# A decoder trunk on one core: dense matmuls in closed runs of twelve

## The chip, the cores and the metric

The kernel runs on one core of a Trainium2 chip. The metric is the device time of one execution in microseconds, the median of several runs. TensorE multiplies matrices into PSUM banks; VectorE, ScalarE and GpSimd compute elementwise; SyncE issues the DMAs that bring the weights.

## What is computed

The reference is a trunk of two residual layers, each followed by a dense FFN, over 512 tokens of width 1024 in float32. Cut to its frame:

```python
for i in range(DEPTH):                      # DEPTH = 2
    if i % 2 == 0:                          # SSD heads and GLA heads from one input projection
        h = rms_norm(x, mix_norm_even[j])
        proj = h @ w_in                     # z, xbc, dt, q, k, v, g, gk_low
        x = x + concat(ssd_mixer(...), gla_mixer(...)) @ w_out
    else:                                   # multi-head latent attention, 16 heads, causal
        h = rms_norm(x, mix_norm_odd[j])
        x = x + mla_layer(h, w_dqkv, ..., w_o)
    x = x + (silu(h2 @ w_gate) * (h2 @ w_up)) @ w_down     # h2 = rms_norm(x, ffn_norm[i])
```

The SSD part has 16 heads of 64 with chunks of 128 tokens, the GLA part 4 heads with chunks of 64, the hidden width of the FFN is 2816.

## The kernel before

The activations lie transposed, width on the 128 partitions and the 512 tokens along the free axis, so x is eight tiles X[0..7]. A float32 product is made of three matmuls in a reduced type (`mm3`, L149 to L152): operand and weight are each split into a high and a low part, and high x high (L150), low operand x high weight (L151) and high operand x low weight (L152) are summed in one PSUM bank. `dense` (L154) does this for the eight k tiles of a product, which makes 24 matmuls 128x512 into one bank `acc`. Of these banks there are NACC = 3, taken in turn, so the fourth product after a given one has to wait until that one's bank was read out.

Weights come one block of 512 KB at a time: a DMA into `wraw` (2 buffers), a cast on ScalarE into the high part `whi` (L144), a subtraction on VectorE into the low part `wlo` (L145); whi and wlo have 3 buffers each. `weight` (L130) asks for them under a raised priority of AHEAD = 90.

The order of every engine's instructions is set by the Tile scheduler: it goes by priority, which falls in the order of the program and is raised inside `tc.high_priority(offset=...)`, and by its own estimate of when inputs are there. Products therefore interleave: while a dense product runs, small matmuls of other parts (transposes, scores of a chunk, sums over partitions) can stand between any two of its 24.

The places that the prediction goes through:

- `rstd` (L173 to L197) makes the factor R of a norm. The squares are split (L178, L179), two matmuls with a matrix of ones sum them over the partitions (L181 and L182), and then VectorE works through L186 to L196. All evacuations of the FFN's gate and up products need R (L680, L683).
- `out_round(r)` (L267) adds one quarter of the output product of the first layer, with four parts mxh/mxl as operands. The second quarter takes the SSD's second group, normalized by `group_norm` (L460): y = y x gain x Rg (L464), then a cast mxh (L126) and a subtraction mxl (L127). It is called inside the first GLA head, ahead of that head's scores (L594).
- `conv` (L351) of the SSD part evacuates its product at L358; the recursion dp (L322) shares VectorE with it.
- `attend` (L898) does two heads: scores (L911), mask and maximum (L914), exp (L916), reciprocal (L919), scaling (L922), transposes (L925), copies (L929), and the product with the values (L934) after the last copy. `o_round` (L944) is the output product that runs beside the later heads.
- `ffn` (L666): 22 pairs of a gate and an up product, then the down products.

Of the kernel before, what the change touches and what calls it, by code (L numbers as in the profile page):

```python
# [21 lines left out]
KD = 8  # L22
HID = 2816
KH = HID // P
EPS = 1e-6
AHEAD = 90
VALUES = (2, 3, 7)
SC = 4
NACC = 3
# [17 lines left out]
def kernel(ctx: ExitStack, tc: tile.TileContext, A, yT, stop=99):  # L47
    nc = tc.nc
    V, S, G, E = nc.vector, nc.scalar, nc.gpsimd, nc.tensor
# [47 lines left out]
    ps = acc()  # L97
# [48 lines left out]
        return (hi[:, :kc * m].rearrange("p (k m) -> p k m", k=kc),  # L146
                lo[:, :kc * m].rearrange("p (k m) -> p k m", k=kc))

    def mm3(out, ah, al, bh, bl, first, last):  # L149
        E.matmul(out, ah, bh, start=first, stop=False)  # L150
        E.matmul(out, ah, bl, start=False, stop=False)  # L151
        E.matmul(out, al, bh, start=False, stop=last)  # L152

    def dense(ps, w, xs):  # L154

        n = len(xs)
        for k, (xh, xl) in enumerate(xs):
            mm3(ps, w[0][:, k, :], w[1][:, k, :], xh, xl, k == 0, k == n - 1)

    def rsqrt(pool, m, shape, tag, ytag=""):  # L160

# [124 lines left out]
    with tc.tile_pool(name="gkp", bufs=1) as gkp:  # L286
        rtok = tok_scalar(R)

        ps = aux("a1")
# [15 lines left out]
        ps = aux()  # L305
# [40 lines left out]
        with tc.tile_pool(name="ssd", bufs=2) as sp:  # L346
# [123 lines left out]
            def values(h):  # L470

                wv = [weight(A["w_v"][h, j], 4, 256) for j in range(2)]
                v = gkp.tile([P, 4, 256], F32, name=f"v{h}")
                for i in range(4):
                    ps = acc()
                    for k in range(KD):
                        wh, wl = wv[k // 4]
                        xh, xl = xp[k]
                        mm3(ps[:, :256], xh[:, i * P:(i + 1) * P], xl[:, i * P:(i + 1) * P],
                            wh[:, k % 4, :], wl[:, k % 4, :], k == 0, k == KD - 1)  # L480
                    S.activation(v[:, i, :], ps[:, :256], AF.Copy, scale=rtok[:, i:i + 1])
                vt[h] = v

# [229 lines left out]
    with tc.tile_pool(name="mla", bufs=2) as mp, tc.tile_pool(name="mla1", bufs=1) as m1:  # L713
# [112 lines left out]
        def project(g):  # L826


            qs = mp.tile([P, 4, 4, 96], F32, tag="qs", name=nm("qs"))
            wqs = [weight(A["w_uq"][g, :, k0:k0 + n], n, 384) for k0, n in ((0, 2), (2, 1))]  # L830
            for i in range(4):
                ps = acc()
                for k in range(3):
                    lh, ll = lora["q"][k]
                    wh, wl = wqs[k // 2]
                    mm3(ps[:, :384], lh[:, i * P:(i + 1) * P], ll[:, i * P:(i + 1) * P],
                        wh[:, k % 2, :], wl[:, k % 2, :], k == 0, k == 2)
                S.activation(qs[:, i].rearrange("p h d -> p (h d)"), ps[:, :384], AF.Copy,
                             scale=cf["q"][:, i:i + 1])

            wkv = weight(A["w_ukv"][g], 2, 512)
            ks = mp.tile([P, 4, 4, 64], F32, tag="ks", name=nm("ks"))
            v = mp.tile([P, 4, 4, 64], F32, tag="v", name=nm("v"), bufs=3)
            for i in range(4):
                ps = acc()
                for k in range(2):
                    lh, ll = lora["kv"][k]
                    mm3(ps, lh[:, i * P:(i + 1) * P], ll[:, i * P:(i + 1) * P],
                        wkv[0][:, k, :], wkv[1][:, k, :], k == 0, k == 1)
                p3 = ps.rearrange("p (w h d) -> p w h d", w=2, h=4)  # L850
                S.activation(ks[:, i], p3[:, 0], AF.Copy, scale=cf["kv"][:, i:i + 1])
                S.activation(v[:, i], p3[:, 1], AF.Copy, scale=cf["kv"][:, i:i + 1])

            sq = mp.tile([P, 16, 96], F32, tag="sq", name=nm("sq"), bufs=1)
            st = mp.tile([P, 3, 16], F32, tag="st", name=nm("st"))
            S.activation(sq, qs.rearrange("p i h d -> p (i h) d"), AF.Square)
            V.tensor_reduce(st[:, 0], sq[:, :, 0:64], AX.X, ALU.add)
            V.tensor_reduce(st[:, 1], sq[:, :, 64:96], AX.X, ALU.add)
            S.activation(sq[:, :, 0:64], ks.rearrange("p i h d -> p (i h) d"), AF.Square)
            V.tensor_reduce(st[:, 2], sq[:, :, 0:64], AX.X, ALU.add)  # L860
            for j, n in enumerate((64, 32, 64)):
                V.tensor_scalar(st[:, j], st[:, j], 1.0 / n, EPS, ALU.mult, ALU.add)
            rf = rsqrt(mp, st, [P, 3, 16], "hr")
            q2 = qs.rearrange("p i h d -> p (i h) d")
            V.tensor_tensor(q2[:, :, 0:64], q2[:, :, 0:64],
                            rf[:, 0].unsqueeze(2).to_broadcast([P, 16, 64]), ALU.mult)
            rr = mp.tile([P, 16, 32], F32, tag="rr", name=nm("rr"), bufs=1)
            V.tensor_tensor(rr, q2[:, :, 64:96],
                            rf[:, 1].unsqueeze(2).to_broadcast([P, 16, 32]), ALU.mult)
            rope(qs[:, :, :, 64:96], rr.rearrange("p (i h) d -> p i h d", i=4), tabs[0], [P, 4, 4, 32])  # L870
            k2 = ks.rearrange("p i h d -> p (i h) d")
            V.tensor_tensor(k2, k2, rf[:, 2].unsqueeze(2).to_broadcast([P, 16, 64]), ALU.mult)
            return qs, ks, v
# [184 lines left out]
```

## Time and profile before

| | |
|---|---|
| median of 3 runs | 1372.63 us (1371.01 to 1373.25) |
| the profiled execution's own time | 1371.09 us |
| its span | 1368.9 us |
| TensorE busy | 1344.9 us, 98% |
| VectorE busy | 815.5 us, 60% |
| ScalarE busy | 562.8 us, 41% |

The span is what the trace covers; the time of the execution has some two microseconds around it. Matmuls overlap in the records, so that TensorE's time is read from the distance of one start to the next and not from a record's length. The program in stages, by the trace: the SSD part until about 240 us, GLA heads and output product until 410, the first FFN until 775, the attention layer's projections until 835, its heads until 992, the output product until about 1005, then the second FFN.

### The profile page before, as it was taken

How to read it: one execution, taken by the hardware profiler on the slowest of the kernel's cores; microseconds unless marked ns; L12 is line 12 of the kernel's file. 1: busy time of each engine (PE TensorE's matmuls, PEld its weight loads, DVE VectorE, ACT ScalarE, POOL GpSimd, SP SyncE). 2: the span in 40 equal slices, each digit the busy share in tenths (PEclk: the TensorE clock that was granted, in tenths of full speed). 3: DMA queues.
4: the chain of work that ended last, by engine and by line, in shares of the span. 5: the costliest groups of instructions: out<-in, count | busy, mean ns of one | idle time of the engine just before them, and what ended most of it. 6: DMA issues, size and time to landing. Idle time of an engine off the chain costs nothing.

```text
span 1368.9 us, 16667 instructions
## 1 busy us (share of the span) xinstructions
PE 1344.9 (98%) x6506; PEld 1088.7 (80%) x6506; DVE 815.5 (60%) x1369; ACT 562.8 (41%) x941; POOL 7.8 (1%) x35
## 2 busy tenths in 40 slices
PE   8999999999999999999999999999999999999998
PEld 5788889788888888888888887666588888888887
DVE  7987976788867444444333469776594444443221
ACT  5584633544344322332232348775653322322121
POOL 0000000000000000000000000000000000000000
PEclk9999999999999999999999999999999999999999
DMA  5342232222233333223333321111033223323331
GB/s 177 109 141 91 77 95 78 78 77 62 79 93 105 93 94 106 92 92 99 90 100 100 101 68 56 39 47 62 1 98 103 93 93 102 98 93 108 111 103 63
DMA packets 36781, 122.22 MB, mean 89 GB/s; under 512 B 4768, under 2 KB 5792, under 8 KB 36704
## 3 DMA queue, kind: packets, MB, share of 16 engines
q1 hardware_dynamic: 35888, 120.72, 28.1%
q8 instruction: 51, 0.84, 0.2%
q10 hardware_dynamic: 816, 0.46, 0.1%
q14 instruction: 26, 0.21, 0.0%
HBM read 119.03 MB, written 2.13 MB: 89 GB/s over the span
## 4 chain that ended last, share of the span: by engine, by line
PE 90%; DVE 5%; ACT 3%; issue 1%; DMA 1%; SPq 0%; ACTq 0%
PE acc L150 27%; PE acc L151 27%; PE acc L152 27%; PE sco L911 2%; PE ptr L925 1%; PE po L934 1%; DVE wlo L145 1%; PE a L447 1%; PE a L625 0%; PE a L433 0%; PE a L614 0%; PE a L451 0%; ACT whi L144 0%; PE a L627 0%; DVE gm L534 0%
## 5 line engine op out<-in xcount | busy, mean ns | idle before, releaser
L150 PE MATMUL acc<-xh,whi 128*128 128x512 f32 x1144 | 449.1, 393 | 5.2 <-DVE dp L322 2.5
L144 ACT CAST whi<-wraw 128x1024 fp32r<-128x1024 f32 (+2 forms) x221 | 225.8, 1022 | 554.0 <-PE acc L151 436.9
L151 PE MATMUL acc<-xl,whi 128*128 128x512 f32 x1144 | 448.7, 392 | 0.0
L152 PE MATMUL acc<-xh,wlo 128*128 128x512 f32 x1144 | 448.7, 392 | 0.0
L145 DVE TENSOR_TENSOR wlo<-wraw,whi 128x1024 fp32r<-128x1024 f32 (+2 forms) x221 | 261.9, 1185 | 163.2 <-ACT whi L144 163.1
L150 PEld LDWEIGHTS acc<-xh,whi 128*128 128x128 f32 x1144 | 214.9, 188 | 51.2 <-ACT cvt L366 2.8
L152 PEld LDWEIGHTS acc<-xh,wlo 128*128 128x128 f32 x1144 | 215.1, 188 | 44.8 <-DVE wlo L145 0.6
L151 PEld LDWEIGHTS acc<-xl,whi 128*128 128x128 f32 x1144 | 215.1, 188 | 44.5 <-issue 1.4
L152 PE MATMUL acc<-fhh,wlo 128*128 128x512 f32 x288 | 112.0, 389 | 0.0
L150 PE MATMUL acc<-fhh,whi 128*128 128x512 f32 x288 | 112.0, 389 | 0.0
L151 PE MATMUL acc<-fhl,whi 128*128 128x512 f32 x288 | 112.0, 389 | 0.0
L683 DVE TENSOR_TENSOR fu<-acc,R 128x512 f32<-128x512 f32 x44 | 30.4, 691 | 136.2 <-PE acc L152 136.2
L680 DVE TENSOR_TENSOR fg<-acc,R 128x512 f32<-128x512 f32 x44 | 30.4, 691 | 89.0 <-PE acc L152 88.9
L152 PEld LDWEIGHTS acc<-fhh,wlo 128*128 128x128 f32 x288 | 54.1, 188 | 11.3
L151 PEld LDWEIGHTS acc<-fhl,whi 128*128 128x128 f32 x288 | 54.1, 188 | 11.3
L150 PEld LDWEIGHTS acc<-fhh,whi 128*128 128x128 f32 x288 | 54.1, 188 | 11.1
L151 PE MATMUL acc<-mxl,whi 128*128 128x512 f32 x128 | 49.9, 391 | 0.0
L150 PE MATMUL acc<-mxh,whi 128*128 128x512 f32 x128 | 49.8, 391 | 0.0
L152 PE MATMUL acc<-mxh,wlo 128*128 128x512 f32 x128 | 49.7, 390 | 0.0
L911 PE MATMUL sco<-kT,qT 96*128 96x128 f32 (+3 forms) x128 | 42.8, 445 | 1.5 <-DVE mx L914 1.3
L914 DVE CUSTOM_DVE_ANT_0 sc<-sco,am 128x128 f32<-128x128 f32 (+3 forms) x64 | 30.7, 487 | 13.6 <-PE sco L911 11.5
L916 ACT ACTIVATE sc<-sc,mx 128x128 f32<-128x128 f32 (+3 forms) x64 | 35.7, 561 | 7.3 <-DVE mx L914 6.8
(329 smaller groups left out, 1584.8 us busy)
## 6 DMA issues: line engine op xcount, KB each, us to landing
wraw<-in_w_gate_dram SPq DMA_DIRECT2D x44, 512.0 KB, 3.5
wraw<-in_w_up_dram SPq DMA_DIRECT2D x44, 512.0 KB, 3.5
wraw<-in_w_down_dram SPq DMA_DIRECT2D x32, 512.0 KB, 3.6
wraw<-in_w_out_dram SPq DMA_DIRECT2D x16, 512.0 KB, 3.6
wraw<-in_w_xbc_dram SPq DMA_DIRECT2D x12, 512.0 KB, 3.6
wraw<-in_w_down_dram SPq DMA_DIRECT2D x16, 384.0 KB, 3.1
wraw<-in_w_z_dram SPq DMA_DIRECT2D x8, 512.0 KB, 3.5
wraw<-in_w_v_dram SPq DMA_DIRECT2D x8, 512.0 KB, 3.5
```

The lines of the kernel that those rows point to most:

```text
L144: S.copy(hi[:, :kc * m], r)
L145: V.tensor_tensor(lo[:, :kc * m], r, hi.bitcast(F32)[:, :kc * m], ALU.subtract)
L150: E.matmul(out, ah, bh, start=first, stop=False)
L151: E.matmul(out, ah, bl, start=False, stop=False)
L152: E.matmul(out, al, bh, start=False, stop=last)
L447: E.matmul(pd[64 * h:64 * h + 64, c * P:(c + 1) * P], xdt[:, c, h, :], mt[:, h, c, :], start=True, stop=True)
L680: V.tensor_tensor(g, pg, R, ALU.mult)
L683: V.tensor_tensor(u, pu, R, ALU.mult)
L911: E.matmul(ps[:, :n], qts[j][:, b * P:(b + 1) * P], kts[j][:, :n], start=True, stop=True)
L914: V.tensor_tensor_reduce(sc[:, :n], ps[:, :n], am[:, T - n:], -scale, 3e38, ALU.add, ALU.min, mx[:, j:j + 1])
L916: S.activation(sc[:, :n], sc[:, :n], AF.Exp, bias=mx[:, j:j + 1], scale=-1.0, accum_out=sm[:, j:j + 1])
L925: E.transpose(ps[:, kb * P:(kb + 1) * P], sc[:, kb * P:(kb + 1) * P], ident)
```

## The change

Two constants come in, and `mm3` gets an argument `close`. Its second and third matmul are always issued under a priority raised by 5000, its first one too if `close` is set. `dense` sets it for all k but each fourth (RUN = 4), so that a run of four k tiles, twelve matmuls, is taken as a whole once its first matmul has been placed; the values of the GLA part (L479) do it by four, the q and kv products of the attention layer (L836, L848) over all their k. The FFN's down product calls `mm3` without the argument.

```diff
--- before.py
+++ after.py
@@ -24,6 +24,8 @@
 KH = HID // P
 EPS = 1e-6
 AHEAD = 90
+CLOSE = 5000
+RUN = 4
 VALUES = (2, 3, 7)
 SC = 4
 NACC = 3
@@ -146,16 +148,19 @@
         return (hi[:, :kc * m].rearrange("p (k m) -> p k m", k=kc),
                 lo[:, :kc * m].rearrange("p (k m) -> p k m", k=kc))
 
-    def mm3(out, ah, al, bh, bl, first, last):
-        E.matmul(out, ah, bh, start=first, stop=False)
-        E.matmul(out, ah, bl, start=False, stop=False)
-        E.matmul(out, al, bh, start=False, stop=last)
+    def mm3(out, ah, al, bh, bl, first, last, close=False):
+
+        with tc.high_priority(offset=CLOSE if close else 0):
+            E.matmul(out, ah, bh, start=first, stop=False)
+        with tc.high_priority(offset=CLOSE):
+            E.matmul(out, ah, bl, start=False, stop=False)
+            E.matmul(out, al, bh, start=False, stop=last)
 
     def dense(ps, w, xs):
 
         n = len(xs)
         for k, (xh, xl) in enumerate(xs):
-            mm3(ps, w[0][:, k, :], w[1][:, k, :], xh, xl, k == 0, k == n - 1)
+            mm3(ps, w[0][:, k, :], w[1][:, k, :], xh, xl, k == 0, k == n - 1, k % RUN > 0)
 
     def rsqrt(pool, m, shape, tag, ytag=""):
 
@@ -477,7 +482,7 @@
                         wh, wl = wv[k // 4]
                         xh, xl = xp[k]
                         mm3(ps[:, :256], xh[:, i * P:(i + 1) * P], xl[:, i * P:(i + 1) * P],
-                            wh[:, k % 4, :], wl[:, k % 4, :], k == 0, k == KD - 1)
+                            wh[:, k % 4, :], wl[:, k % 4, :], k == 0, k == KD - 1, k % 4 > 0)
                     S.activation(v[:, i, :], ps[:, :256], AF.Copy, scale=rtok[:, i:i + 1])
                 vt[h] = v
 
@@ -834,7 +839,7 @@
                     lh, ll = lora["q"][k]
                     wh, wl = wqs[k // 2]
                     mm3(ps[:, :384], lh[:, i * P:(i + 1) * P], ll[:, i * P:(i + 1) * P],
-                        wh[:, k % 2, :], wl[:, k % 2, :], k == 0, k == 2)
+                        wh[:, k % 2, :], wl[:, k % 2, :], k == 0, k == 2, k > 0)
                 S.activation(qs[:, i].rearrange("p h d -> p (h d)"), ps[:, :384], AF.Copy,
                              scale=cf["q"][:, i:i + 1])
 
@@ -846,7 +851,7 @@
                 for k in range(2):
                     lh, ll = lora["kv"][k]
                     mm3(ps, lh[:, i * P:(i + 1) * P], ll[:, i * P:(i + 1) * P],
-                        wkv[0][:, k, :], wkv[1][:, k, :], k == 0, k == 1)
+                        wkv[0][:, k, :], wkv[1][:, k, :], k == 0, k == 1, k > 0)
                 p3 = ps.rearrange("p (w h d) -> p w h d", w=2, h=4)
                 S.activation(ks[:, i], p3[:, 0], AF.Copy, scale=cf["kv"][:, i:i + 1])
                 S.activation(v[:, i], p3[:, 1], AF.Copy, scale=cf["kv"][:, i:i + 1])
```

No instruction is added or removed. By the order that the scheduler makes, TensorE has 6140 rows before and after, 5376 of them matmuls of dense products. Stretches of other work between dense matmuls are 123 before and 97 after. Before, the runs of dense matmuls between them have lengths of 1 to 25 and more, irregularly; after, 44 of them have exactly 12 and 15 exactly 24. In both FFNs, from the second or third pair on, twelve matmuls of a gate product and twelve of its up product now alternate; before, each product ran its 24 through.

In the rows below a name is a tile with its number; after the change the lines of the code stand two lower up to `dense` and five lower behind it, and mm3's matmuls are L154, L156 and L157.

TensorE at the start of the first FFN, where acc_3851 is the first gate product, acc_3882 the first up product and st_3827 the sum over partitions for R, before:

```order
L150 MATMUL acc_3851<-xh_3809,whi_3847 128x512
L151 MATMUL acc_3851<-xl_3810,whi_3847 128x512
L181 MATMUL st_3827<-rsa_3823,ones_r 128x512
L152 MATMUL acc_3851<-xh_3809,wlo_3848 128x512
L150 MATMUL acc_3882<-xh_3645,whi_3878 128x512
L182 MATMUL st_3827<-rsb_3824,ones_r 128x512
L151 MATMUL acc_3882<-xl_3646,whi_3878 128x512
L152 MATMUL acc_3882<-xh_3645,wlo_3879 128x512
L150 MATMUL acc_3882<-xh_3665,whi_3878 128x512
```

and after; the run of twelve begins three rows further up, right behind the first of the two sums, L186:

```order
L154 MATMUL acc_3851<-xh_3761,whi_3847 128x512
L156 MATMUL acc_3851<-xl_3762,whi_3847 128x512
L157 MATMUL acc_3851<-xh_3761,wlo_3848 128x512
L154 MATMUL acc_3851<-xh_3788,whi_3847 128x512
L156 MATMUL acc_3851<-xl_3789,whi_3847 128x512
L157 MATMUL acc_3851<-xh_3788,wlo_3848 128x512
L154 MATMUL acc_3851<-xh_3809,whi_3847 128x512
L156 MATMUL acc_3851<-xl_3810,whi_3847 128x512
L157 MATMUL acc_3851<-xh_3809,wlo_3848 128x512
L187 MATMUL st_3827<-rsb_3824,ones_r 128x512
L154 MATMUL acc_3882<-xh_3740,whi_3878 128x512
```

Before, the sums stand behind 23 and 25 dense matmuls of this FFN; after, behind 24 and 36.

VectorE where the second round of the output product begins; y_2150, mxh_2193 and mxl_2194 are the last part of the second SSD group, wlo_2483 the low half of this round's first weight, wlo_2517 that of its second, before:

```order
L127 TENSOR_TENSOR mxl_2179<-y_1472,mxh_2178 128x512
L127 TENSOR_TENSOR mxl_2184<-y_1613,mxh_2183 128x512
L127 TENSOR_TENSOR mxl_2189<-y_1755,mxh_2188 128x512
L464 SCALAR_TENSOR_TENSOR y_2150<-y_2150,pv,Rg_2166 128x512
L145 TENSOR_TENSOR wlo_2483<-wraw_2480,whi_2482 128x1024
L127 TENSOR_TENSOR mxl_2194<-y_2150,mxh_2193 128x512
L558 SCALAR_TENSOR_TENSOR qd_2396<-acc_2369,R_188 128x512
L145 TENSOR_TENSOR wlo_2517<-wraw_2514,whi_2516 128x1024
L519 TENSOR_TENSOR gw<-w_2323,wt 16x512
```

and after:

```order
L129 TENSOR_TENSOR mxl_2179<-y_1472,mxh_2178 128x512
L129 TENSOR_TENSOR mxl_2184<-y_1613,mxh_2183 128x512
L129 TENSOR_TENSOR mxl_2189<-y_1755,mxh_2188 128x512
L147 TENSOR_TENSOR wlo_2517<-wraw_2514,whi_2516 128x1024
L469 SCALAR_TENSOR_TENSOR y_2150<-y_2150,pv,Rg_2166 128x512
L129 TENSOR_TENSOR mxl_2194<-y_2150,mxh_2193 128x512
L563 SCALAR_TENSOR_TENSOR qd_2396<-acc_2369,R_188 128x512
L576 TENSOR_TENSOR kr_2433<-acc_2408,R_188 128x512
L524 TENSOR_TENSOR gw<-w_2323,wt 16x512
```

The low half wlo_2517 moved from behind mxl_2194 to before y_2150; on ScalarE the cast of whi_2516 moved in the same way ahead of that of mxh_2193. wlo_2483 now stands further up, ahead of the last step that makes Rg.

TensorE at the end of the last pair of heads; sco are scores, ptr transposed scores, po the product with the values, acc_8295 and acc_8322 products of the output projection, before:

```order
L150 MATMUL acc_8322<-xh_1457_7749,whi_8318 128x512
L151 MATMUL acc_8322<-xl_1458_7750,whi_8318 128x512
L152 MATMUL acc_8322<-xh_1457_7749,wlo_8319 128x512
L150 MATMUL acc_8322<-xh_1519_8017,whi_8318 128x512
L151 MATMUL acc_8322<-xl_1520_8018,whi_8318 128x512
L152 MATMUL acc_8322<-xh_1519_8017,wlo_8319 128x512
L925 MATMUL ptr_8238<-ident,sc_8228 128x128 x4
L925 MATMUL ptr_8245<-ident,sc_8233 128x128 x4
L150 MATMUL acc_8322<-xh_1561_8149,whi_8318 128x512
L151 MATMUL acc_8322<-xl_1562_8150,whi_8318 128x512
L152 MATMUL acc_8322<-xh_1561_8149,wlo_8319 128x512
L934 MATMUL po_8251<-pt_8153,v_7419 64x512
```

and after:

```order
L930 MATMUL ptr_8190<-ident,sc_8180 128x128 x2
L930 MATMUL ptr_8195<-ident,sc_8185 128x128 x2
L916 MATMUL sco_8226<-kT_6532,qT_8033 128x512
L930 MATMUL ptr_8213<-ident,sc_8203 128x128 x3
L930 MATMUL ptr_8219<-ident,sc_8208 128x128 x3
L916 MATMUL sco_8231<-kT_6534,qT_8040 128x512
L930 MATMUL ptr_8238<-ident,sc_8228 128x128 x4
L930 MATMUL ptr_8245<-ident,sc_8233 128x128 x4
L939 MATMUL po_8251<-pt_8153,v_7419 64x512
L939 MATMUL po_8251<-pt_8154,v_7419 64x512
```

The dense matmuls that stood among the transposes and before the values are now all ahead of this piece.

On VectorE at the start of the SSD part, L358 of the third convolution stands after the low half of a weight (wlo_685) and after the first three steps of dp before the change; after it, L358 stands ahead of dp, and that low half behind six steps of dp.

## Rows read from the trace of the kernel before

**Rows 1.** The page: the span, the engines' busy time with its share of the span and the number of their instructions, and the chain of work that ended last, by engine and then by line.

```profile
span 1368.9 us, 16667 instructions
PE 1344.9 (98%) x6506; PEld 1088.7 (80%) x6506; DVE 815.5 (60%) x1369; ACT 562.8 (41%) x941; POOL 7.8 (1%) x35
...
PE 90%; DVE 5%; ACT 3%; issue 1%; DMA 1%; SPq 0%; ACTq 0%
PE acc L150 27%; PE acc L151 27%; PE acc L152 27%; PE sco L911 2%; PE ptr L925 1%; PE po L934 1%; DVE wlo L145 1%; PE a L447 1%; PE a L625 0%; PE a L433 0%; PE a L614 0%; PE a L451 0%; ACT whi L144 0%; PE a L627 0%; DVE gm L534 0%
```

**Rows 2.** The view of waits, TensorE alone: what it stood before, the instruction that ended the wait, the sum in us, how many times, the longest.

```profile
PE acc L150 <- ACT qT L894: 3.0, 2, 1.6
...
PE sco L911 <- DVE mx L914: 1.3, 4, 0.5
```

**Rows 3.** The table by stage: the stretch in us, its length, busy us and instructions of TensorE, of its weight loads, of VectorE, ScalarE and GpSimd, then TensorE's granted clock, the DMA share and GB/s.

```profile
240.00:275.00 35.00, 32.96 (x157) 25.77 (x155) 27.81 (x38) 19.91 (x27) 1.95 (x5) 0.95 0.25 76
...
410.00:775.00 365.00, 365.00 (x1611) 301.88 (x1610) 165.49 (x200) 111.11 (x138) 0.00 (x0) 1.00 0.31 96
```

**Rows 4.** The timeline of TensorE at the start of the first FFN: start us, duration us, engine, line, operation, out<-in, form, and in brackets the idle time before it and what ended that.

```profile
421.20 0.39 PE L151 MATMUL acc<-xl,whi 128*128 128x512 f32 x1
421.47 0.50 PE L181 MATMUL st<-rsa,ones_r 128*128 128x512 f32 x1
421.81 0.39 PE L152 MATMUL acc<-xh,wlo 128*128 128x512 f32 x1
422.04 0.40 PE L150 MATMUL acc<-xh,whi 128*128 128x512 f32 x1
422.28 0.41 PE L182 MATMUL st<-rsb,ones_r 128*128 128x512 f32 x1
422.53 0.39 PE L151 MATMUL acc<-xl,whi 128*128 128x512 f32 x1
...
433.23 0.39 PE L150 MATMUL acc<-xh,whi 128*128 128x512 f32 x1
```

**Rows 5.** The timeline near the start of the program: VectorE's evacuation of a bank, the matmul of TensorE that waits, and a wait later on.

```profile
45.58 0.68 DVE L358 TENSOR_TENSOR xpad<-acc,R 128x512 f32<-128x512 f32 x1
...
46.40 0.47 PE L150 MATMUL acc<-xh,whi 128*128 128x512 f32 x1 [2.46 <-DVE dp L322]
...
89.19 0.91 PE L433 MATMUL a<-xde,btok 128*128 128x128 f32 x6 [0.41 <-DVE xde L428]
```

**Rows 6.** The timeline of VectorE in the same stretch of the first FFN as rows 4.

```profile
422.73 0.69 DVE L186 TENSOR_SCALAR sq<-st 128x512 f32<-128x512 f32 x1 [0.59 <-PE st L182]
...
428.90 1.22 DVE L145 TENSOR_TENSOR wlo<-wraw,whi 128x1024 fp32r<-128x1024 f32 x1
...
431.49 0.69 DVE L680 TENSOR_TENSOR fg<-acc,R 128x512 f32<-128x512 f32 x1
```

**Rows 7.** The timeline at the start of the second FFN, two instructions of TensorE and then three of VectorE.

```profile
1011.91 0.42 PE L182 MATMUL st<-rsb,ones_r 128*128 128x512 f32 x1
...
1022.20 0.40 PE L150 MATMUL acc<-xh,whi 128*128 128x512 f32 x1
...
1012.04 1.23 DVE L145 TENSOR_TENSOR wlo<-wraw,whi 128x1024 fp32r<-128x1024 f32 x1 [0.26 <-ACT whi L144]
1013.18 0.68 DVE L186 TENSOR_SCALAR sq<-st 128x512 f32<-128x512 f32 x1
...
1021.24 0.69 DVE L680 TENSOR_TENSOR fg<-acc,R 128x512 f32<-128x512 f32 x1
```

**Rows 8.** The timeline where the second round of the output product begins: two rows of ScalarE, two of VectorE, one of TensorE.

```profile
238.62 0.62 ACT L126 CAST mxh<-y 128x512 fp32r<-128x512 f32 x1 [1.72 <-DVE y L464]
239.73 1.05 ACT L144 CAST whi<-wraw 128x1024 fp32r<-128x1024 f32 x1 [0.48 <-PE acc L151]
...
237.84 0.74 DVE L464 SCALAR_TENSOR_TENSOR y<-y,pv,Rg 128x512 f32<-128x512 f32 x1
...
239.64 0.68 DVE L127 TENSOR_TENSOR mxl<-y,mxh 128x512 fp32r<-128x512 f32 x1
...
241.98 0.39 PE L151 MATMUL acc<-mxl,whi 128*128 128x512 f32 x1
```

**Rows 9.** The timeline of the last pair of attention heads: two rows of VectorE, two of ScalarE, two of TensorE.

```profile
981.40 0.68 DVE L914 CUSTOM_DVE_ANT_0 sc<-sco,am 128x512 f32<-128x512 f32 x1
...
983.66 0.88 DVE L922 TENSOR_SCALAR sc<-sc,sm 128x512 f32<-128x512 f32 x2
...
982.61 0.74 ACT L916 ACTIVATE sc<-sc,mx 128x512 f32<-128x512 f32 x1
...
984.96 1.07 ACT L929 COPY pt<-ptr 128x512 f32<-128x512 f32 x2 [1.53 <-PE ptr L925]
...
984.29 1.06 PE L925 MATMUL ptr<-ident,sc 128*128 128x128 f32 x8
...
986.09 2.16 PE L934 MATMUL po<-pt,v 128*64 128x512 f32 x12
```

**Rows 10.** The timeline of TensorE behind its wait in the first head of the GLA part.

```profile
265.66 0.27 PE L594 MATMUL a<-qd,ki 128*64 128x64 f32 x1 [1.88 <-DVE ki L575]
...
267.53 0.63 PE L150 MATMUL acc<-xh,whi 128*128 128x512 f32 x1
267.96 0.63 PE L151 MATMUL acc<-xl,whi 128*128 128x512 f32 x1
```

## The prediction

> **What bounds the kernel now.** I read the page's busy shares and its chain first. TensorE is busy 98% of a span of 1368.9 us and makes up 90% of the chain that ended last [rows 1], so the time is the time of TensorE's own instructions plus the moments in which it waits. That leaves 1368.9 - 1344.9 = 24 us in which it is idle, and the largest entry in the view of its waits is 3.0 us [rows 2]. What a change of order can win is bounded by those 24 us and by what a switch between kinds of matmul costs; what it can lose has no such bound. Third, the table by stage: in 410 to 775 us, the first FFN, TensorE is busy 365.00 of 365.00 us at a granted clock of 1.00 [rows 3]. The two FFNs are over half of the program and have nothing to give. What is left are the places where another engine ends the wait, and I went through them in the timeline.
>
> **What the change does.** It removes and adds no instruction; 6140 rows of TensorE stay, 5376 of them dense matmuls. It moves. Stretches of other work between dense matmuls fall from 123 to 97, so 26 entries and exits go. The other side: a small product that used to slip in between any two matmuls of a dense product now comes up to eleven matmuls later, and whoever waits for it with it. The Tile scheduler also lays out VectorE's and ScalarE's queues anew, since it places all engines together.
>
> **Term 1, saved switches.** Dense matmuls start 365.00 / 1611 = 0.227 us apart [rows 3]; the 0.39 that a row records for one overlaps with the next [rows 4]. A switch shows around the two matmuls that sum a norm over the partitions, as wide as a dense one: L151 at 421.20, L181 at 421.47, L152 at 421.81 [rows 4] are two steps in 0.61 where dense ones take 0.45, a loss of 0.16. L150 at 422.04, L182 at 422.28, L151 at 422.53 [rows 4] are two steps in 0.49, a loss of 0.04. So 26 switches are worth between 26 x 0.04 = 1.0 and 26 x 0.16 = 4.2 us; no row says which kind is the commoner, and I take **-2.0**, a little below the middle.
>
> **Term 2, the start.** TensorE stands 2.46 us before the matmul at 46.40, and the row names dp, but what frees its bank is the evacuation L358 that stands among dp's steps on VectorE, 45.58 to 46.26 [rows 5]. In the new order VectorE does that evacuation ahead of a weight's low half (one takes 1.22 us [rows 6]) that stood before it, so at least 1.2 us sooner. That low half now stands behind the recursion dp and may hold up the next product. I estimate **-0.9**, between -1.6 (with two steps of dp that now come later too) and +0.5. At 89.19 L433 waits 0.41 for xde [rows 5]; a whole dense run now stands ahead of it: **-0.4**.
>
> **Term 3, the first FFN's norm.** The chain goes L182 (422.28) [rows 4], L186 (422.73), the nine steps on VectorE that make R, with two low halves between them (one at 428.90), then L680 (431.49, 0.69 us), which empties the first bank [rows 6]. The fourth dense product needs that bank and starts at 433.23 [rows 4]; the bank is free at 432.18, a slack of 1.05 us. Before, L182 stands after 25 dense matmuls of this FFN, after the change behind 36: 11 x 0.227 = 2.5 us later. Nothing in the chain is idle, so the bank comes at 434.7 and TensorE, with all three banks full, waits 2.5 - 1.05 = **+1.45**.
>
> **Term 4, the second FFN's norm.** The same chain: L182 at 1011.91, L186 at 1013.18, L680 at 1021.24 to 1021.93, fourth product at 1022.20 [rows 7]: slack 0.27. L182 moves behind 36 dense matmuls, to about 1013.6. L186 did not wait for it before, it stood behind a low half of a weight (1012.04, 1.23 us [rows 7]); now it starts at about 1014.0, 0.85 later, and that low half stands inside the chain, 1.2 more: 2.0 - 0.27 = **+1.75**.
>
> **Term 5, the second round of the output product.** The fourth k step of its first product needs mxl, done at 239.64 + 0.68 = 240.32, and its second matmul runs at 241.98 [rows 8]: slack 1.66. ScalarE casts mxh at 238.62 and the next weight at 239.73 [rows 8]; after the change the weight comes first, and it can't be cast sooner, since its buffer is freed by the product that ends just then. Its cast (1.05, to 240.8), its low half on VectorE (1.22, to 242.0), which now stands before the last y (0.74 [rows 8]), then mxh (0.62) and mxl (0.68): 244.1 against 241.98, **+2.1**. If VectorE slides past it, 0; if the products behind it wait too, 2.7.
>
> **Term 6, the last pair of attention heads.** From the last scores to their transposes the chain is L914 at 981.40, exp L916 at 982.61, scale L922 at 983.66, L925 at 984.29, then the copies L929 at 984.96 and L934 at 986.09 [rows 9]. Before, fifteen dense matmuls of the output product lie in it. After, nine of these stand earlier and six earlier still, and nothing is left between the last L911 and L934. Even before, that chain left 984.29 - 981.40 = 2.9 us between L914 and L925, of which some 0.4 are a gap behind other work (the end of L914 at 982.1 to L916 at 982.61): some 2.5 us of it can't be shortened. Between L925 and L934 lie 986.09 - 984.29 = 1.8, of which L925 itself takes 0.83 (the 1.06 of its row overlap with what follows): some 0.85 for the copies. Without cover **+3.4**. The six matmuls moved up may fill a wait there (mx 1.3 [rows 2]): down to +1.5.
>
> **What costs nothing.** In both FFNs gate and up now alternate by twelve. A weight is then needed for a second product while the first still runs, and its buffer's slack falls from 48 matmuls (10.9 us) to 24 (5.4). A weight's cast takes 1.05 us [rows 8], its low half 1.22 [rows 6]; with the waits between an estimated 2.6 us, which lie inside 5.4, so I cost it at nothing. The 1.88 us at L594 [rows 10] stay: 60 dense matmuls lie between the start of its chain (L527) and L594, before and after.
>
> **The clock.** After the wait that ends at 265.66 the matmuls of 267.53 and 267.96 and four more are 0.43 apart, not 0.227 [rows 10], and the granted clock of that stretch is 0.95 [rows 3]: a drop from 2.4 to 1.2 GHz that costs 6 x 0.2 = 1.2 us. The wait of 2.46 us at 46.40 [rows 5] was followed by no such matmuls. The Trainium skill, TensorE: Matmul & The Clock Gate, Loop structure matters more than you think, says that matmuls issued back to back keep the clock up and idle gaps between bursts drop it. By it longer runs would save the drop and the sum would be +4.2 instead of +5.4; but the gap before 265.66 comes from VectorE, and the run before it is as long after the change, so by the trace nothing is saved. What the change makes are three longer gaps: I put no drop for them in the sum; two drops are a rival.
>
> **Sum.** -2.0 - 0.9 - 0.4 + 1.45 + 1.75 + 2.1 + 3.4 = +5.4. Against the profiled execution's 1371.09 us that is 1376.5; the median of the runs, 1372.63, is 1.5 above that execution, so on its footing 1378.0. I say **1377**.
>
> **Rivals.**
> - *The covers hold (ends faster).* VectorE and ScalarE run ahead wherever TensorE loses a little earlier, so the added waits are eaten by existing ones, and terms 1 and 2 alone are left: -3.3, with all switches at their full price -5.5: 1367 to 1369. For it: VectorE is busy only 60% [rows 1]. Against: in the norms' chains no step waits for anything but the step before it [rows 6, 7], so a later L182 comes out whole. It decides from added waits below 0.5 us together. Chance 0.20.
> - *Half of it.* Terms 3 and 4 come, 5 and 6 slide: -3.3 + 3.2 = 0, so 1371 to 1375. Chance 0.25.
> - *Drops of the clock on top.* Two of the three new waits over 1.7 us draw one each: +2.4, 1380. Chance 0.15.
> - *Alternating gate and up starves a weight.* If a new weight comes 0.3 us late in each of some 40 pairs, +12: 1389. Against it: 2.8 us of slack, worked out above, and three banks in turn cost nothing now, at a clock of 1.00 [rows 3]. The Trainium skill, TensorE: Matmul & The Clock Gate, A second HAM failure mode: psum-queue depth-cycling, tells of a kernel that lost its clock by going round its banks each iteration; the trace's FFN goes round three and shows no loss, so I leave it at 0.05.
>
> **How the numbers follow.** The sum as it stands has 0.35. A difference below 0.2% (2.7 us) can't be told from none: faster is below 1369.9, slower above 1375.4. Faster 0.20, same 0.25, slower 0.35 + 0.15 + 0.05 = 0.55. The range reaches from the first rival's middle, 1368, to 1382 (1378.0 on the median's footing, with two drops, 2.4, term 5's upper end, 0.6, and 1 for term 1's lower end); outside stay the starving case, half of the first rival and a little of the third, together under 0.2. The slower cases alone would be 1375.5 to 1382.
>
> **What the profile after would show.** Term 3: TensorE waiting for L680's release before the fourth product of the first FFN, 1 to 2 us; term 4 the same in the second. Term 5: a wait for mxh or mxl at the first product of the second output round. Term 6: waits named sc and pt before L925 and L934 at the end of attention. Term 2: the wait for dp below 2 us. The forecast is wrong if these four waits are absent, if waits stand in the FFN's steady part (TensorE not at 365 of 365 us there), or if dense starts come closer than 0.227 us, so that the switches were worth more than any row shows.

## The result

The changed kernel takes 1378.48 us (median of 5 runs, 1377.26 to 1380.17) against 1373.25 us (5 runs) for the kernel before on the same chip: a ratio of 1.0044, 95% interval 1.003 to 1.0058, so 5.2 us slower. 1377 was predicted, in a range of 1368 to 1382. The profiled execution's span grew from 1368.9 [rows 1] to 1375.4 us, by 6.5.

The page of the changed kernel: span, busy time of the engines, the chain by engine.

```profile
span 1375.4 us, 16667 instructions
PE 1347.1 (98%) x6506; PEld 1093.5 (80%) x6506; DVE 815.7 (59%) x1369; ACT 564.3 (41%) x941; POOL 7.8 (1%) x35
...
PE 85%; DVE 9%; ACT 3%; issue 1%; DMA 1%; SPq 0%; ACTq 0%; DVEq 0%
```

The instructions and their number are those of before; VectorE's share of the chain rose from 5% to 9%. That tells where to look, not how much is lost, since a chain counts the work behind a wait and not the wait alone. By the two pages TensorE's idle time (the span less its busy time) grew from 24.0 to 28.3 us, which is 4.3 of the 6.5; its busy time grew by the other 2.2. The view of waits names the places (the sum in us, how many, the longest):

```profile
PE acc L154 <- DVE fg L685: 3.3, 2, 1.8
PE ptr L930 <- DVE sc L927: 3.2, 3, 2.5
...
PE acc L154 <- ACT mxh L128: 1.5, 1, 1.5
...
PE po L939 <- ACT pt L934: 0.7, 1, 0.7
```

The rows of fg, mxh and pt L934 are new; that of sc stood at 0.6 us, one wait, before. fg is the first evacuation of either FFN (L680 before), sc and pt belong to the last pair of heads, mxh to the second output round. The view counts idle time from the end of the record ahead, and a dense record lasts 0.39 us where the next one would start after 0.227 [rows 3, 4], so behind a dense matmul each wait costs 0.16 us more than it shows. The wait of 2.46 us at 46.40 [rows 5] shrank to 0.64, at 44.67 now. The timeline of TensorE at these places (start, duration, instruction, and in brackets the wait ahead of it):

```profile
44.67 0.47 PE L154 MATMUL acc<-xh,whi 128*128 128x512 f32 x1 [0.64 <-DVE da L322]
...
240.61 0.50 PE L154 MATMUL acc<-mxh,whi 128*128 128x512 f32 x1 [1.52 <-ACT mxh L128]
...
241.34 0.50 PE L156 MATMUL acc<-mxl,whi 128*128 128x512 f32 x1 [0.23 <-DVE mxl L129]
...
433.37 0.47 PE L154 MATMUL acc<-xh,whi 128*128 128x512 f32 x1 [1.78 <-DVE fg L685]
...
986.55 1.77 PE L930 MATMUL ptr<-ident,sc 128*128 128x128 f32 x8 [2.45 <-DVE sc L927]
...
989.00 4.54 PE L939 MATMUL po<-pt,v 128*64 128x512 f32 x16 [0.68 <-ACT pt L934]
994.22 0.96 PE L154 MATMUL acc<-xh,whi 128*128 128x512 f32 x3 [0.69 <-ACT xh L128]
...
1028.70 0.47 PE L154 MATMUL acc<-xh,whi 128*128 128x512 f32 x1 [1.50 <-DVE fg L685]
```

The durations of the two rows at 986.55 and 989.00 are to be seen too. Before, the same eight transposes took 1.06 us [rows 9], and the sixteen records of the product with the values, of which [rows 9] shows twelve, took 2.38:

```profile
986.09 2.38 PE L934 MATMUL po<-pt,v 128*64 128x512 f32 x16
```

Now it is 1.77 and 4.54. The table by stage of the changed kernel (stretch, length, TensorE's busy us and instructions, granted clock, DMA share, GB/s) tells why:

```profile
240.00:250.00 10.00, 9.16 (x30) 0.83 0.23 60
...
260.00:275.00 15.00, 13.13 (x64) 1.00 0.13 40
410.00:775.00 365.00, 363.22 (x1602) 1.00 0.30 94
985.00:990.00 5.00, 2.77 (x12) 0.68 0.00 0
990.00:995.00 5.00, 4.31 (x19) 0.64 0.00 0
```

Behind the wait of 2.45 us the clock stood at 0.68 and 0.64 on the mean of ten us, that is at 1.2 GHz for most of them. The first FFN lost 1.78 us of its 365, all in the one wait; its steady part, with gate and up alternating, runs as before.

### The profile page after: what moved, and what is told of

It reads as the page before. It is cut to its first block, busy times and chain, and to the rows that moved or that the text cites. A ratio compares the mean times of both kernels' runs of the same rounds, so it can differ in the third digit from the quotient of the medians.

```text
span 1375.4 us, 16667 instructions
## 1 busy us (share of the span) xinstructions
PE 1347.1 (98%) x6506; PEld 1093.5 (80%) x6506; DVE 815.7 (59%) x1369; ACT 564.3 (41%) x941; POOL 7.8 (1%) x35
## 4 chain that ended last, share of the span: by engine, by line
PE 85%; DVE 9%; ACT 3%; issue 1%; DMA 1%; SPq 0%; ACTq 0%; DVEq 0%
PE acc L154 26%; PE acc L157 25%; PE acc L156 25%; PE sco L916 2%; DVE wlo L147 2%; PE po L939 1%; PE ptr L930 1%; PE a L452 1%; ACT whi L146 1%; DVE cva L368 1%; PE a L630 1%; DVE sc L919 0%; PE a L438 0%; ACT sc L921 0%; PE a L456 0%
## 5 line engine op out<-in xcount | busy, mean ns | idle before, releaser
L154 PE MATMUL acc<-xh,whi 128*128 128x512 f32 x1144 | 451.1, 395 | 6.7 <-DVE fg L685 3.3
L157 PE MATMUL acc<-xh,wlo 128*128 128x512 f32 x1144 | 445.9, 390 | 0.3 <-DVE wlo L147 0.3
L156 PE MATMUL acc<-xl,whi 128*128 128x512 f32 x1144 | 445.6, 390 | 0.0
L154 PEld LDWEIGHTS acc<-xh,whi 128*128 128x128 f32 x1144 | 214.7, 188 | 54.3 <-ACT whi L146 4.2
L157 PEld LDWEIGHTS acc<-xh,wlo 128*128 128x128 f32 x1144 | 214.8, 188 | 45.8 <-DVE wlo L147 0.7
L156 PEld LDWEIGHTS acc<-xl,whi 128*128 128x128 f32 x1144 | 214.8, 188 | 44.8 <-DVE xl L129 0.9
L157 PE MATMUL acc<-fhh,wlo 128*128 128x512 f32 x288 | 112.0, 389 | 0.0
L154 PE MATMUL acc<-fhh,whi 128*128 128x512 f32 x288 | 112.0, 389 | 0.0
L156 PE MATMUL acc<-fhl,whi 128*128 128x512 f32 x288 | 112.0, 389 | 0.0
L154 PEld LDWEIGHTS acc<-fhh,whi 128*128 128x128 f32 x288 | 54.1, 188 | 11.3
L157 PEld LDWEIGHTS acc<-fhh,wlo 128*128 128x128 f32 x288 | 54.1, 188 | 11.2
L156 PEld LDWEIGHTS acc<-fhl,whi 128*128 128x128 f32 x288 | 54.1, 188 | 11.1
L154 PE MATMUL acc<-mxh,whi 128*128 128x512 f32 x128 | 51.3, 403 | 1.5 <-ACT mxh L128 1.5
L156 PE MATMUL acc<-mxl,whi 128*128 128x512 f32 x128 | 50.5, 396 | 0.3 <-DVE mxl L129 0.2
L157 PE MATMUL acc<-mxh,wlo 128*128 128x512 f32 x128 | 50.5, 395 | 0.0
```

## The experiments

**1 and 2. What a switch costs.** On the kernel before, small products that nobody reads were added in the FFNs, 44 times one transpose in the first, 44 times a pair of products on half of the array's columns in the second; scattered, one behind each product:

```diff
+            spare = aux()
                 dense(pg, w, xp)
+                if layer == 0:
+                    E.transpose(spare[:, :P], ident, ident)
+                else:
+                    E.matmul(spare[64:P, :P], ident[:, 0:64], ident, start=True, stop=True)
+                    E.matmul(spare[0:64, :P], ident[:, 64:P], ident, start=True, stop=True)
                 ...
                 dense(pu, w, xp)
+                (the same again)
```

> The kernel before, with extra small products whose results nobody reads: in the first FFN one 128x128 transpose behind each gate and each up product (44 of them, each between two dense runs), in the second FFN at the same places a pair of 128x128 products on half the columns of the array (64 wide). The theory of the prediction prices a switch from dense matmuls to a small product and back at 0.04 to 0.16 us, so the first FFN takes 44 x 0.11 = 4.9 us for the transposes themselves and 2 to 7 us for the switches, more than before. The rival, that a switch is dear and that fewer of them are the change's real gain, wants 0.3 us and more each, 13 us and more.

and gathered, all 44 in a row behind the eleventh pair (`for _ in range(44 if c == 10 else 0)`):

> The kernel before with the same 44 transposes in the first FFN and the same 44 pairs of half-width products in the second, but all 44 in one row behind the eleventh pair, so that there is one switch instead of 44. The theory: FFN longer than before by the bare work alone, about 4.9 us in the first; the difference to the scattered version divided by 43 is the price of one switch, 0.04 to 0.16 us. The rival: a difference of 13 us and more.

Scattered took 1405.77, gathered 1385.88 us, one run each. The timelines give it for each FFN: the second sum of the norm and the first matmul behind the FFN (or the last of all). Scattered:

```profile
424.54 0.43 PE L182 MATMUL st<-rsb,ones_r 128*128 128x512 f32 x1
...
784.16 0.39 PE L758 MATMUL acc<-xh,w 128*96 128x512 f32 x1
...
1020.14 0.42 PE L182 MATMUL st<-rsb,ones_r 128*128 128x512 f32 x1
...
1399.39 0.39 PE L152 MATMUL acc<-fhh,wlo 128*128 128x512 f32 x1
```

Gathered:

```profile
422.30 0.43 PE L182 MATMUL st<-rsb,ones_r 128*128 128x512 f32 x1
...
780.81 0.39 PE L754 MATMUL acc<-xh,w 128*96 128x512 f32 x1
...
1016.77 0.43 PE L182 MATMUL st<-rsb,ones_r 128*128 128x512 f32 x1
...
1379.51 0.39 PE L152 MATMUL acc<-fhh,wlo 128*128 128x512 f32 x1
```

First FFN: 359.62 against 358.51 us, so 1.11 / 43 = 0.026 us for a switch to a transpose and back. Second: 379.25 against 362.74, so 16.51 / 43 = **0.38 us** for a switch to products on half the columns. The expected 0.04 to 0.16 was missed at both ends: the first figure is below it, the second is what the rival wanted. One such switch in the scattered kernel, where each of the two products appears as two records:

```profile
1103.95 0.39 PE L152 MATMUL acc<-xh,wlo 128*128 128x512 f32 x1
1104.27 0.32 PE L680 MATMUL st<-ident 128*64 128x128 f32 x1
...
1104.64 0.50 PE L150 MATMUL acc<-xh,whi 128*128 128x512 f32 x1
1104.98 0.39 PE L151 MATMUL acc<-xl,whi 128*128 128x512 f32 x1
```

From 1103.95 the half-width pair starts after 0.32 instead of 0.227, the dense matmul behind it starts another 0.37 later, where gathered pairs are 0.22 apart, and the next one after 0.34: entry and exit both cost. The half-width products differ from the transposes in a second way, they are products. That isn't what costs, as a place in the kernel before shows, where products on the full array stand between dense matmuls:

```profile
47.17 0.39 PE L150 MATMUL acc<-xh,whi 128*128 128x512 f32 x1
47.39 1.05 PE L378 MATMUL a<-cT,bT 128*128 128x128 f32 x8
...
48.52 0.40 PE L152 MATMUL acc<-xh,wlo 128*128 128x512 f32 x1
```

Two dense steps and eight records that are 0.11 us apart in a row make 0.45 + 0.88 = 1.33; the rows take 1.35. The Trainium skill, TensorEngine Tiling (Array Packing), Tiling Modes, Key Properties, says that a change of the tiling mode drains the engine; the runs fit that and give the cost here. So the kind of the stretch decides what a bare switch is worth, and the orders tell the kinds: 26 stretches before hold half-width products (L447, L594 to L596, L934), 25 after. Of the 26 stretches that the change saves, one is of the dear kind. 25 x 0.026 + 0.38 = 1.0 us, for small products that wait for nothing, as the added ones; those of the program can come late besides (term 1 below).

**3. Is the slow end of attention the wait or the clock?** The changed kernel with ten matmuls put into the wait, into the bank that the values will use:

```diff
             po = aux("po")
+            if 2 * g + hp == 7:
+                for _ in range(10):
+                    E.matmul(po, ones_r, oparts[0][0], start=True, stop=True)
```

> The changed kernel with ten extra matmuls 128x512 in the last pair of heads, written into the bank of the product with the values before that product starts and not read; by the order they stand between the last scores and the last transposes, in the stretch where TensorE waits 2.45 us. They take 10 x 0.227 = 2.27 us of that wait and change no dependency. The theory: the slow transposes and values behind that wait (granted clock 0.66, about 3 us lost) come from the idle time before them, so the clock stays at 1.00 there, the last L930 x8 and L939 run at their old pace, and the kernel is 2 to 3 us faster than the changed kernel, 1375 to 1376, though it does more work. The rival, that the clock falls for another reason, or that the waits alone are the loss: no change, 1378 to 1379.

Measured: 1377.51 us (10 runs, 1373.82 to 1379.41), ratio to the kernel before 1.0021 (1.0009 to 1.0033). By the medians that is only 1.0 us less than the changed kernel, not the 2 to 3 that were expected, so the total doesn't settle it; why it gained less is not shown. The place itself does. The timeline of TensorE there:

```profile
983.64 2.90 PE L939 MATMUL po<-xh,ones_r 128*128 128x512 f32 x10
986.65 1.06 PE L930 MATMUL ptr<-ident,sc 128*128 128x128 f32 x8
988.44 2.37 PE L942 MATMUL po<-pt,v 128*64 128x512 f32 x16 [0.73 <-ACT pt L934]
991.50 0.98 PE L154 MATMUL acc<-xh,whi 128*128 128x512 f32 x3 [0.69 <-ACT xh L128]
```

and the table by stage, with the granted clock as the third column from the end:

```profile
985.00:990.00 5.00, 4.16 (x24) 1.00 0.00 0
990.00:995.00 5.00, 4.32 (x25) 1.00 0.00 0
```

The transposes still start at 986.65, so what they need from VectorE comes no sooner; the values take 2.37 instead of 4.54, and the clock stays at 1.00. From the transposes to the next dense matmul it is 991.50 - 986.65 = 4.85 us, in the changed kernel 994.22 - 986.55 = 7.67. The end of attention therefore holds two losses, 3.1 us of waits and 2.8 us of clock, and the second goes when ten dense matmuls stand in the place of the idle time.

**4. Does alternating gate and up cost anything?** The changed kernel with the FFN's gate and up products at an offset of 0; by the order they then alternate by three matmuls:

```diff
-        with tc.high_priority(offset=CLOSE if close else 0):
+        with tc.high_priority(offset=CLOSE if close and on else 0):
 ...
-        with tc.high_priority(offset=CLOSE):
+        with tc.high_priority(offset=CLOSE if on else 0):
 ...
-                dense(pg, w, xp)
+                dense(pg, w, xp, False)          # and the same for pu
```

> The changed kernel, but the gate and up products of both FFNs get an offset of 0 in place of 5000; by the order gate and up then alternate by three matmuls instead of twelve, so TensorE changes its bank four times as often, and both weights of a pair are in use until its end. The theory: changing the bank costs nothing at all, and any loss is a wait for a weight, which needs a buffer that is freed only at the end of the pair (cast 1.05, low half 1.22, then TensorE): up to 1 us for each of 44 pairs where the cover of a few matmuls is too short, named as a wait for wlo or whi. The rival, that alternating banks itself slows matmuls or the clock: dense starts farther apart than 0.227 us with no wait named, or a granted clock below 1.00 in the steady part.

One run, 1377.2 us. The table by stage, FFNs only:

```profile
600.00:775.00 175.00, 175.00 (x773) 1.00 0.31 94
1030.00:1180.00 150.00, 150.00 (x663) 1.00 0.29 95
```

TensorE is busy all the time at full clock, 175.00 / 773 = 0.226 us for a matmul. Neither the banks nor the weights cost anything there, even at four times the changes. The wait for fg is gone as well, since the sums slip in early again. The total of this one run says less: it is only 1.3 us below the changed kernel's, though 3.3 us of waits for fg are gone, and its profile shows a granted clock of 0.83 in 870 to 880 us, where the changed kernel's shows 1.00.

**5. The sums of the norm.** The changed kernel with only the two sums raised above the closed runs:

```diff
-        E.matmul(ps, ones_r, hi, start=True, stop=False)
-        E.matmul(ps, ones_r, lo, start=False, stop=True)
+        with tc.high_priority(offset=2 * CLOSE):
+            E.matmul(ps, ones_r, hi, start=True, stop=False)
+            E.matmul(ps, ones_r, lo, start=False, stop=True)
```

> The changed kernel with the two matmuls that sum a norm over the partitions at a still higher priority (twice 5000), so that they may stand inside a run of twelve. By the order the second sum stands behind 26 dense matmuls of the first FFN instead of 36 and behind 28 instead of 36 in the second, and in front of the second output round 1.3 us of dense work earlier, with the low half of the next weight again behind mxl. The theory, that the late sums alone make the waits before the fourth product of either FFN (1.78 and 1.50 us) and the wait for mxh and mxl (1.75 us): these waits are gone or below 0.3 us, the kernel is 4 to 5 us faster than the changed kernel, about 1373.5 to 1374.5, ratio to the kernel before 1.000 to 1.002; the waits at the end of attention stay. The rival, that the waits in the FFNs come from alternating gate and up: they stay, 1378.

1372.32 us (10 runs), ratio 0.9992 (0.9982 to 1.0001); that is 1.2 us below the lower end of what was expected, and where the surplus comes from is not shown. Two matmuls of each norm were raised, and the waits for fg and mxh are gone from the list. The first FFN in the table by stage:

```profile
410.00:775.00 365.00, 364.99 (x1610) 1.00 0.32 96
```

and a row of its view of waits:

```profile
PE st L538 <- ACT gw L532: 1.3, 1, 1.3
```

The row of gw is new: at the second output round the next thing in the order is now what comes late, so of the 1.75 us there only some 0.4 are won.

**6. The output product of attention.** The changed kernel with o_round's matmuls issued as before (for `on=False`, mm3 issues the three without raised priority):

```diff
                     dense(ps, (w[0][:, :, j * P:(j + 1) * P], w[1][:, :, j * P:(j + 1) * P]),
-                          oparts[4 * r:4 * r + 4])
+                          oparts[4 * r:4 * r + 4], False)
```

> The changed kernel with the output product of the attention layer (o_round) as before, its matmuls without raised priority. By the order the last pair of heads again has fifteen dense matmuls among its scores, transposes and values. The theory: the waits before the last L925 and L934 (2.45 and 0.68 us) and the low clock behind them (some 3 us) go, and with them about 5 us; what the closed runs saved earlier in attention, about 1 us, goes too: 1373 to 1374.5, ratio 1.000 to 1.002. The rival, that closing saves switches worth 0.3 us each beside the heads (six stretches more): only 3 us faster.

1373.14 us (10 runs), ratio 1.0 (0.9989 to 1.001). Its timeline at the end of attention:

```profile
986.51 1.06 PE L935 MATMUL ptr<-ident,sc 128*128 128x128 f32 x8
...
988.30 2.37 PE L944 MATMUL po<-pt,v 128*64 128x512 f32 x16
```

There is no wait in either row, and the durations are the old ones. With the dense matmuls among the transposes, 1378.48 - 1373.14 = 5.3 us by the medians came back. fg and mxh still wait in this kernel, as they should.

**7. A longer run, as a test of the sums' place.** RUN = 8 in place of 4, so that all 24 stay together.

> The changed kernel with RUN = 8: a dense product's 24 matmuls stay together. By the order the stretches of other work fall from 96 to 81, gate and up don't alternate, and the second sum of the norm stands behind 48 dense matmuls in both FFNs instead of 36. The theory, that the place of the sum sets the wait: 12 x 0.227 = 2.7 us more at each FFN, waits of 4.5 and 4.2 us there, the end of attention as in the changed kernel; fifteen switches fewer, of which two to four on half of the array at 0.38 us, save 1 to 2 us: 1381 to 1384, ratio 1.006 to 1.009, and more if a wait of over 4 us draws a low clock. The rival, that longer runs are better in themselves and the loss was the alternation: faster than the changed kernel, 1376 or less.

1383.53 us (4 runs), ratio 1.0076 (1.0063 to 1.009), and the view of waits has

```profile
PE acc L154 <- DVE fg L685: 8.4, 2, 4.2
```

Twelve dense matmuls more ahead of the second sum make 4.2 us of wait in either FFN, where 4.5 and 4.2 were worked out. Gate and up don't alternate here, so the loss isn't theirs.

**8. All of it mended.** Sums first; o_round, the second output round (`r != 1`) and the FFNs' gate and up without raised priority; closed runs stay in the input projections and the other output rounds.

> The changed kernel with the sums of the norms first (as in sums_first), and the output product of the attention layer, the second output round and both FFNs' gate and up products without raised priority, so that closed runs are left in the input projections of the SSD, GLA and attention parts and in the other output rounds. The theory: what the change won before the first FFN (about 3.5 us without the wait for mxh) stays and every added wait goes: 1367 to 1369.5 on the footing of a median of 1372.6, ratio 0.996 to 0.998. The rival, that the gain at the start is bound to the later waits (the scheduler only moves a wait from one place to the other): ratio 1.000 or above.

1365.20 us (5 runs), ratio **0.994** (0.9928 to 0.9953): 8.6 us faster than the kernel before beside it (1373.77), and more than expected. The table by stage tells where the surplus is:

```profile
240.00:275.00 35.00, 33.65 (x165) 1.00 0.25 76
```

The clock of this stretch was 0.95 before [rows 3], with a wait of 1.88 us at L594 [rows 10]. Both are gone. The chain to ki starts at the last of four small products (L527 before, L538 here). This kernel, and then that of experiment 5, which still waits at the same place (L594 is L605 in both):

```profile
250.39 0.42 PE L538 MATMUL st<-gx,gw 80*128 80x512 f32 x1
...
266.28 0.27 PE L605 MATMUL a<-qd,ki 128*64 128x64 f32 x1
```

```profile
251.71 0.40 PE L538 MATMUL st<-gx,gw 80*128 80x512 f32 x1
...
267.68 0.27 PE L605 MATMUL a<-qd,ki 128*64 128x64 f32 x1 [1.91 <-DVE ki L586]
```

From row to row it is 15.9 and 16.0 us. But here 68 dense matmuls stand between the two, by the trace, where the other kernels have 60; eight more are 8 x 0.227 = 1.8 us, and with them ki is no longer late. In this execution the drop of the clock is gone with the wait. That is 1.9 + 1.2 = 3.1 us that the expectation had left in place.

## Why the prediction was right, point by point

**Term 1, saved switches (-2.0): right in direction, but the price was not that of a switch.** It was put at 0.04 to 0.16 us each from one kind of stretch; experiments 1 and 2 show two kinds of bare switch, 0.026 and 0.38 us, outside that range at either end, and the kinds of the 26 give -1.0. More than that was saved where stretches begin. A small product that comes up to 0.16 us late leaves no wait in the view. By the starts in the trace (the step from the last dense matmul to the first small product, less 0.227 for a dense step of 512 columns, listed waits included, stretches of low clock left out), these delays add up to 12.0 us over 120 entries before and to 5.7 over 95 after. So the longer runs also took away delays, which the prediction had at L433 only; that operands had more time to arrive is the likely reason, not a shown one. That its price came out between the two counts is luck.

**Term 2, the start (-0.9 and -0.4): right in direction, too small.** The wait shrank from 2.46 to 0.64, -1.8; the low half that was to hold up the next product makes no wait there (the one wait of 0.3 us for a wlo that the view shows stands at 146.86). L433's wait is gone from that view.

**Terms 3 and 4, the norms' sums (+1.45, +1.75): right.** 1.78 and 1.50 us, 0.16 more each by the starts, at the fourth product of either FFN (with three banks, the first product's bank comes round again three products later, not four), and by the mechanism named: experiment 5 takes the waits away by moving the sums alone, experiment 7 makes them grow by the dense matmuls put ahead, experiment 4 shows that the alternation has no part in it.

**Term 5, the second output round (+2.1): right in size, in part by luck.** 1.52 for mxh and 0.23 for mxl, 1.75. The low half does stand ahead of the last y. But the next weight was cast at 236.86, not at 239.73 or later, so the step "it can't be cast sooner" failed, and mxl was done at 241.28 instead of 244.1 (the term's own figures add up to 244.04):

```profile
236.86 1.05 ACT L146 CAST whi<-wraw 128x1024 fp32r<-128x1024 f32 x1
240.59 0.69 DVE L129 TENSOR_TENSOR mxl<-y,mxh 128x512 fp32r<-128x512 f32 x1 [0.68 <-ACT mxh L128]
```

For that the product was ready for its fourth k step 2.8 us sooner, at 238.93 (0.227 behind the matmul of 238.70) instead of 241.75: from the second sum of the group's norm to the product's first matmul it was 14.9 us before (224.84 to 239.71) and 12.6 after (223.90 to 236.46), since 60 dense matmuls lie between instead of 79, by the trace. The late sum, which the term did not have, is thus part of the wait; two errors met. Experiment 5, which raises the sums, takes the wait away, but puts the low half behind mxl again too, so it doesn't part the two.

**Term 6, the last heads (+3.4): right.** 2.45 and 0.68, 3.1; experiment 6 undoes it.

**The clock (0 in the sum, +2.4 as a rival with 0.15): this step was the weak one.** The drop behind the last heads costs 2.8 us by experiment 3. The price of one drop was taken from the six slow matmuls at 267.53 [rows 10], 1.2 us; here the clock stayed low for most of ten us, with a second wait of 0.68 inside them. A drop behind 240.61 came on top (clock 0.83 in 240 to 250), while the one behind L594 was absent in this execution (1.00 in 260 to 275). The Trainium skill, TensorE: Matmul & The Clock Gate, Loop structure matters more than you think, has it that matmuls kept back to back hold the clock and a long wait between them drops it; experiment 3 agrees, with 0.64 to 0.68 behind the gap and 1.00 when it was filled, though not every wait here drew a drop (last section).

**What does not add up.** The added waits, 1.78 + 1.50 + 1.75 + 3.13 = 8.2, and the drop at the end, 2.8, make 11.0 us; the span grew by 6.5. So 4.5 us were saved on balance. Bare switches and term 2 give 1.0 + 1.8 + 0.4 = 3.2; the delays where stretches begin fell by 6.3, L433's 0.4 among them, which is more than is needed. Against it stand smaller losses: the drop behind 240.61, waits that grew at the start of attention (from 0.55 to 1.23 us at 836, and a new one of 0.67 at 866), and a start of the program in which dense matmuls are 0.43 apart up to 10.5 us, in this execution and not in that of the kernel before. No run separates these. The total was met in part because the terms left too small, the savings and the clock, stand on opposite sides: that is luck.

**The rivals.** That the covers hold (faster) falls: in experiments 5 and 6 each wait is seen to be real. That terms 5 and 6 slide (half of it) falls with the rows of mxh, sc and pt. The starving weights fall by experiment 4, with no wait in the FFNs' steady part. That going round the banks loses the clock falls by the same run, at 1.00 in the FFNs' stretches.

## What to carry to other kernels

Keeping a long product together wins little by the bare switch where its neighbours run on the full array (0.026 us), and can lose up to the length of the run for each small product on which another engine's chain depends. So close the runs, but give the few small products that start a chain (here the sums) a priority above them, and leave products open, as fillers, where a chain would otherwise stand bare; here the two together turned +0.4% into -0.6%. In pricing a wait of one and a half microseconds and more on TensorE, allow for the drop of the clock that may follow it (2.8 us here at the most).

## What the hardware showed that was not expected

A switch between dense matmuls and products on half of the columns costs 0.38 us, fifteen times the 0.026 us of a switch to transposes on the full array. And a wait does not always draw a drop of the clock: the wait before L594, 1.9 us in the kernel before, in the changed one and in that of experiment 3, is followed by 0.89 in the first, 1.00 in the second, and 0.89 in the third, while the wait for mxh, of 1.5 to 1.6 us in the last two, is followed by 0.83 and by 1.00. Nor does it depend on the code alone. The gathered kernel of experiment 2 runs the same instructions as the kernel before up to its first FFN, with the same two waits, and has the drop at the other one. Rows of the table by stage, of the kernel before (the wait of 2.46 us ends at 46.40, that of 1.88 at 265.66):

```profile
40.00:60.00 20.00, 17.54 (x90) 1.00 0.26 95
260.00:275.00 15.00, 13.12 (x71) 0.89 0.13 37
```

and of the gathered one:

```profile
40.00:60.00 20.00, 17.51 (x82) 0.91 0.20 58
260.00:275.00 15.00, 13.18 (x77) 1.00 0.10 37
```

What decides between them stays open. That the wait at 46.40 was followed by no slow matmuls, as the prediction has it, holds for that one execution only. Each such drop is worth 1.2 us and more; the medians of the kernel before, as more of its runs came in, lay between 1372.63 and 1374.55.
